# A planner that counts on its late loads three microseconds later: a one-core hybrid encoder layer

## The chip, the core and the metric

The kernel runs on one core of a Trainium2 chip. The metric is the time of one execution in microseconds on the device. A core has five engines that matter here, each with its own in-order queue of instructions: TensorE (PE), ScalarE (ACT), VectorE (DVE), GpSimd (POOL), and SyncE (SP), which in this kernel issues nearly all DMAs. An instruction that waits for a semaphore holds everything behind it on its engine.

## What is computed

One encoder layer on 512 tokens of width 1024, all in float32. The sizes are D = 1024, 16 heads of 64, a grid of 8 rows of 64 columns, a window of 8 by 16.

```python
mod = silu(c) @ w_c + b_c;  shift, scl, gate = split(mod, 3)
h = rms_norm(x, g_pre) * (1 + scl) + shift
xa, za, q, k, v, zb, ga, gb = split(h @ w_in, 8)
xa = centred_dwconv(xa, conv_w, conv_b)
y_a = ((rg_lru(xa, forward) + rg_lru(xa, backward)) * silu(za)) @ w_pa
y_b = (neighbourhood_attention(q, k, v, rpb) * silu(zb)) @ w_pb
merged = sigmoid(ga) * y_a + sigmoid(gb) * y_b
out = rms_norm(x + gate * (merged @ w_o), g_final)
```

rg_lru makes two block-diagonal sigmoid gates from xa and runs a linear scan over the tokens. The attention adds a relative-position bias and takes a softmax over the 128 keys of each query's window.

## The kernel before

Every large product is computed as three float32r matmuls: each operand is split in a high part (a cast) and a low part (the difference), and high by high, high by low and low by high are summed in one PSUM bank. So a weight tile of 128 x 1024 passes through five steps: SP loads it (wraw, 512 KB), ACT casts it (whi), POOL or DVE subtracts (wlo), PE runs 24 matmuls with it into a bank called acc, and ACT or DVE read acc. This is one projection (`proj`, L684), counted by n. Projections 9 to 32 are q, k and the gate of the eight head pairs, three each, so 12 to 14 belong to the second pair; 33 to 64 belong to four groups of the recurrent branch and of w_pb; 65 to 80 are the merge; then comes w_o.

The value columns are computed first (tiles hx). They are split, written to a scratch tensor in DRAM (vscr) and loaded again in another layout (vt), one group of loads for each two head pairs. An attention of a pair consists of scores on PE (sp), the bias added with a running minimum on DVE (p, mn; the bias tile nb is made on POOL from braw), exp on ACT (p), transposes on PE (pt), the high copy on ACT (pp, L819) and its low part on DVE (pp, L821), the product with vt on PE (pv), and three steps that take pv out (vp on ACT, vp and yt on DVE). The inverse sums (rc) are transposed on PE (mi), copied (rct), written to DRAM (rscr, L863) and loaded again spread over the partitions (rcx, L866), for the factor sz on DVE (L867).

Nothing of this order is written by hand, apart from the head of the program. Every step is recorded with an engine (or a choice of two), an estimated cost, a rank and its tiles, and a planner (`Plan`, L95 to L306) then places one step after another: it keeps a clock for each engine, estimates when each ready step could begin, and takes the one of the lowest rank that can begin within a small window of the earliest. The result is the program order of each engine. What the planner believes about a DMA is in `commit`: the transfers form one stream of 385 GB/s, and a load is there 1.9 us after its share of the stream ends (L222 and L223). What reads it is ready at that end plus the step's own `late` and a lag between engines (L239):

```python
d.t = max(d.t, end + o.late + min(self.lag(e, f) for f in d.alts) if o in d.data else s)
```

`late` moves only the moment from which readers may be placed. It changes neither the stream, nor the time at which a buffer is free. Before, only the parameters (1.9) and the two rcx loads (1.0) have a `late`.

The rank of a weight's load is n - 5, that of the bias and of the gates' weights 4 below the projection at which they stand, that of the vt loads 8 + 6g - 1.5 for the g-th group of values. A load may also be tied to the beginning of an earlier projection (`gate_of`, L681): the weight of projection n to the first matmul of n - 5.

Of the kernel before, what the change touches and what calls it, by code (L numbers as in the profile page):

```python
# [13 lines left out]
P = 128  # L14
# [14 lines left out]

NS, NW = 36, 32  # L30
WARM = 60
LIMITS = {"hx": 8, "acc": 3, "sp": 4, "pt": 2, "pv": 2, "mi": 2, "hd": 3, "gt": 4}


# [295 lines left out]
def layer(ctx, tc, x, x_t, par, w_m, w_g, bc_gate, w_v, w_in, w_blk, rpb, amask, w_pa, w_pb, w_o, g_final, out):  # L330
    nc = tc.nc
# [4 lines left out]
    dp = ctx.enter_context(tc.tile_pool(name="dp", bufs=1, space=bass.MemoryType.DRAM))  # L336
    pl = Plan({"s": NS, "w": NW, "bank": 8}, LIMITS)

    def op(eng, cost, fn, rank, name="", **kw):
        return pl.op(eng, cost, fn, HEAD.get(name, rank), name=name, **kw)  # L340
# [7 lines left out]
    def T(name, dt=F32):  # L348
        return pl.tile("s", lambda i: sb.tile([P, S], dt, tag=f"s{i}", name=nm(name)))
# [9 lines left out]
    def B(cls):  # L359
        return pl.tile(cls, lambda i: ps.tile([P, 512], F32, tag=f"b{i}", name=nm(cls)))  # L360
# [7 lines left out]
    def load(t, dst, src, rank, size, after=(), spare=0, r=(), late=0.0, name="load"):  # L368

        return op("SP", 0.45, lambda e: nc.sync.dma_start(dst(), src() if callable(src) else src), rank,  # L370
                  r=r, w=[t], after=after, spare=spare, size=size, late=late, name=name)

    def cast(o, i):

# [17 lines left out]
    def const(name, shape, dt=F32):  # L392
# [18 lines left out]
       r=[par_sb, ident], w=[pp0])  # L411
# [55 lines left out]
    for i in range(2):  # L467
        for j in range(4):
            load(xTp[j, i], whole(xTp[j, i]), x_t[i, j], -19.9 + 0.4 * i + 0.1 * j, 262144, name=f"x{i}{j}")

    rx = [C("rx", 2) for _ in range(2)]
    for i in range(2):
        st, qs = B("hd"), []
        for j in range(4):
            q = T("sq")
            qs.append(q)
            rank = -17 + 0.4 * i + 0.1 * j
            op("ACT", act(512), lambda e, i=i, j=j, q=q: nc.scalar.activation(q.ap, xTp[j, i].ap, AF.Square), rank,
               r=[xTp[j, i]], w=[q], name=f"sq{i}{j}")
            if j:  # L480
                op(("DVE", "POOL"), (dve(512), pool_(512)), lambda e, a=qs[0], q=q: ENGINE[e].tensor_tensor(a.ap, a.ap, q.ap, op=ALU.add),
                   rank, r=[q], rw=[qs[0]], lock=True, name=f"sqa{i}{j}")
# [14 lines left out]
    def fill(until, wb):  # L497
        for j in range(WARM):
            op("PE", 0.3, lambda e: nc.tensor.matmul(wb.ap[:, :P], onesc.ap, onesc.ap, start=True, stop=True), 5000 + j,
               r=[onesc], hold=[wb], until=until, name="fill")  # L500
# [10 lines left out]
    for i in range(2):  # L511
        op("ACT", act(256), cast(lambda i=i: rbs.ap[:, 256 * i:256 * i + 256], lambda i=i: rb[i].ap[:, :256]), -1 + 0.4 * i,
           r=[rb[i]], w=[rbs.part()], name=f"rbs{i}")
# [4 lines left out]
    def wv_load(k):  # L518
        if k == 0:
            for n in range(2):  # L520
                t = T("wv")
                wv[k, n] = t, (lambda t=t: t.ap)
                load(t, whole(t), w_v[k, :, n * 512:(n + 1) * 512], -17.5, 262144, spare=4, name=f"wv{k}{n}")
        else:
            t = W("wv")
            for n in range(2):
                wv[k, n] = t, (lambda t=t, n=n: t.ap[:, n * 512:(n + 1) * 512])
            load(t, whole(t), w_v[k], k - 4.5, 524288, spare=2, name=f"wv{k}")
# [226 lines left out]
    def attention(pr, q, k, z, nbt, pos):  # L755
# [24 lines left out]
        def half(bs):  # L780
# [77 lines left out]
        rct, rcx = T("rct"), T("rcx")  # L858
        scr = pl.fixed(dp.tile([8, P], F32, name=f"rscr{pr}"))
        op("PE", 0.15, lambda e: nc.tensor.transpose(rcb.ap[:8, :P], rc.ap, ident.ap), pos - 0.3, r=[rc, ident], w=[rcb], name="rcb")  # L860
        op("ACT", 0.3, lambda e: nc.scalar.activation(rct.ap[:8, :P], rcb.ap[:8, :P], AF.Copy, scale=0.5), pos - 0.3, r=[rcb], w=[rct],
           name="rct")
        op("SP", 0.5, lambda e: nc.sync.dma_start(scr.ap, rct.ap[:8, :P]), pos - 3, r=[rct], w=[scr], size=4096, name="rcs")  # L863
        for h in range(2):
            src = bass.AP(scr.ap.tensor, scr.ap.offset + h * P, [[0, 64], [2 * P, 4], [1, P]])
            load(rcx, lambda h=h: rcx.ap[H[h], :].rearrange("p (b q) -> p b q", b=4), src, pos - 3, 131072, r=[scr], name="rcl", late=1.0)  # L866
# [7 lines left out]
           name="ybl")  # L874
# [31 lines left out]
    for pr in range(8):  # L906
        n0 = len(main)
        nbt = bias(pr, n0, gate_of(n0, 2) if pr else [main[6]])
        if pr % 2 == 0:
            load_v(pr // 2, gate_of(n0, 2) if pr else [])  # L910
        q = proj(w_in[16 + pr], hhl, hll, LO_A if pr else "DVE")
        k = proj(w_in[24 + pr], hhl, hll, LO_A)
        z = proj(w_in[32 + pr], hhl, hll, LO_A)
        attention(pr, q, k, z, nbt, k[0] + 0.6)
# [199 lines left out]
    for k in range(KD):  # L1114
        raw, hi, lo = W("wo"), W("woh", F32R), W("wol", F32R)
        rank = n1 - 3 + 0.1 * k
        load(raw, whole(raw), w_o[k * P:(k + 1) * P, :], rank - 2, 524288, after=gate_of(n1, 4), spare=2, name="wo")
        for n in range(2):
            v = lambda n=n, raw=raw: raw.ap[:, n * 512:(n + 1) * 512]
            op("DVE", dve(512), lambda e, n=n, v=v: nc.vector.tensor_tensor(v(), v(), gate[n].ap, op=ALU.mult), rank,  # L1120
               r=[gate[n]], rw=[raw], lock=True, name="wog")
# [59 lines left out]
    pos = [B("acc") for _ in range(NT)]  # L1181
# [8 lines left out]
    for t in range(NT):  # L1190
        for h in range(1 + (t == NT - 1)):
            w = 256 if t == NT - 1 else 512
# [92 lines left out]
```

## Time and profile before

| what | us |
|---|---|
| median of 3 runs | 566.64 |
| lowest and highest | 566.6, 568.99 |
| the profiled execution, its own time | 569.44 |
| its span, first to last instruction | 567.6 |

The profile describes one execution. Its own time is 1.8 us longer than its span, and 2.8 us above the median. Tiles are named without their buffer numbers. A line such as L381 is that of a helper (all three-pass matmuls), so groups are told apart by their tiles. Idle time in brackets is that of the engine directly before the instruction, with what ended it. PE's instructions are pipelined: a matmul of 512 columns is listed with some 390 ns, but the next begins 0.23 us after it.

### The profile page before, as it was taken

The page shows a single profiled execution, that of the slowest core. Times are in us where ns is not written, and L with a number is a line of the kernel's source. Part 1 is how long each engine was busy: PE and PEld are TensorE (multiplying, and loading weights), DVE is VectorE, ACT ScalarE, POOL GpSimd, SP SyncE. Part 2 cuts the span into 40 slices and gives each one's busy share as a digit, 9 for nine tenths or more (in the row PEclk, how much of TensorE's full clock was granted, in tenths as well). Part 3 has the DMA queues.
Part 4 walks back from the last instruction along what each step waited for, and adds up shares of the span by engine and source line. Part 5 has one row for each costly group of instructions (what it writes and reads, how often), then busy time and mean ns, then how long its engine had stood idle before and what let it go on. Part 6 is the DMA issues. An engine that isn't in the chain of part 4 may idle for free.

```text
span 567.6 us, 7658 instructions
## 1 busy us (share of the span) xinstructions
PE 555.9 (98%) x2781; PEld 459.3 (81%) x2781; DVE 388.4 (68%) x696; ACT 322.4 (57%) x568; POOL 100.7 (18%) x95
## 2 busy tenths in 40 slices
PE   8999997999999999999999999999999999999995
PEld 8788886888888888887887887787788888888885
DVE  5899754665576667886489559749847996398323
ACT  6442545557466557579938867984894433234133
POOL 1103539184454550000000000000000000000220
PEclk9999998999999999999999999999999999999999
DMA  8993896652824721305222222223239813380002
GB/s 303 410 401 97 316 270 190 188 148 62 256 56 116 219 88 64 130 13 210 82 104 94 93 83 103 75 74 112 74 106 320 278 38 112 116 329 1 1 37 112
DMA packets 35580, 83.47 MB, mean 147 GB/s; under 512 B 3615, under 2 KB 10967, under 8 KB 35543
## 3 DMA queue, kind: packets, MB, share of 16 engines
q1 hardware_dynamic: 35264, 82.66, 44.1%
q8 instruction: 22, 0.36, 0.3%
q10 hardware_dynamic: 279, 0.32, 0.2%
q14 instruction: 15, 0.12, 0.1%
HBM read 76.65 MB, written 6.32 MB: 146 GB/s over the span
## 4 chain that ended last, share of the span: by engine, by line
PE 89%; DMA 7%; SPq 2%; DVE 1%; ACT 1%; issue 0%; ACTq 0%
PE acc L381 74%; PE hx L381 6%; DMA wv<-in_w_v_dram 3%; PE pv L381 3%; PE gt L381 2%; PE pt L813 2%; PE sp L381 2%; DMA vt<-vscr 2%; DMA wraw<-in_w_in_dram 1%; SPq L370 1%; DMA xT<-in_x_t_dram 1%; SPq L675 1%; DVE va L672 0%; DVE vl L378 0%; ACT vh L375 0%
## 5 line engine op out<-in xcount | busy, mean ns | idle before, releaser
L381 PE MATMUL acc<-hhl,whi 128*128 128x512 f32 x784 | 247.2, 396 | 0.0
L381 PEld LDWEIGHTS acc<-hhl,whi 128*128 128x128 f32 x784 | 143.8, 189 | 30.1 <-issue 1.8
L381 PE MATMUL acc<-hhl,wlo 128*128 128x512 f32 x392 | 153.5, 392 | 0.0
L381 PEld LDWEIGHTS acc<-hhl,wlo 128*128 128x128 f32 x392 | 73.9, 188 | 16.1
L375 ACT CAST whi<-wraw 128x1024 fp32r<-128x1024 f32 x72 | 74.2, 1045 | 9.1 <-DMA wraw<-in_w_in_dram 8.1
L378 POOL TENSOR_TENSOR wlo<-wraw,whi 128x1024 fp32r<-128x1024 f32 x23 | 56.5, 2457 | 73.2 <-ACT whi L375 39.0
L378 DVE TENSOR_TENSOR wlo<-wraw,whi 128x1024 fp32r<-128x1024 f32 x49 | 59.3, 1220 | 14.2 <-ACT whi L375 13.7
L1151 POOL TENSOR_TENSOR yo<-yo,gfin 128x512 f32<-128x512 f32 x6 | 8.2, 1360 | 338.0 <-ACT xr L1148 338.0
L381 PE MATMUL acc<-woh,mhl 128*128 128x512 f32 (+1 forms) x144 | 40.4, 365 | 0.0
L381 PE MATMUL acc<-yahl,whi 128*128 128x512 f32 x128 | 39.4, 389 | 0.0
L381 PE MATMUL acc<-ybhl,whi 128*128 128x512 f32 x128 | 39.4, 389 | 0.0
L1028 DVE SCALAR_TENSOR_TENSOR gm<-gm,acc 128x512 f32<-128x512 f32 x16 | 11.0, 688 | 39.4 <-PE acc L381 39.4
L799 DVE CUSTOM_DVE_ANT_0 p<-sp,nb 128x192 f32<-128x192 f32 (+1 forms) x64 | 32.7, 610 | 6.1 <-PE sp L381 6.1
L730 POOL TENSOR_TENSOR nb<-msk,braw 128x192 f32<-128x192 f32 (+1 forms) x48 | 29.0, 635 | 31.9 <-DMA braw<-in_rpb_dram 31.9
L381 PE MATMUL hx<-vh,hhl 128*128 128x512 f32 x112 | 33.7, 390 | 0.0
L806 ACT ACTIVATE p<-p,mn 128x192 f32<-128x192 f32 (+1 forms) x64 | 30.4, 478 | 5.1 <-DVE mn L799 5.0
L821 DVE TENSOR_TENSOR pp<-pt,pp 128x384 fp32r<-128x384 f32 (+1 forms) x32 | 19.8, 624 | 18.3 <-ACT pp L819 18.2
L381 PEld LDWEIGHTS acc<-woh,mhl 128*128 128x128 f32 x144 | 26.1, 189 | 4.4
L381 PEld LDWEIGHTS acc<-yahl,whi 128*128 128x128 f32 x128 | 24.0, 188 | 5.0
L381 PEld LDWEIGHTS acc<-ybhl,whi 128*128 128x128 f32 x128 | 24.0, 188 | 5.0
L381 PE MATMUL acc<-wol,mhl 128*128 128x512 f32 (+1 forms) x72 | 26.3, 365 | 0.0
L381 PE MATMUL acc<-yahl,wlo 128*128 128x512 f32 x64 | 24.9, 389 | 0.0
(202 smaller groups left out, 954.5 us busy)
## 6 DMA issues: line engine op xcount, KB each, us to landing
wraw<-in_w_in_dram SPq DMA_DIRECT2D x56, 512.0 KB, 5.8
wc<-in_w_m_dram SPq DMA_DIRECT2D x14, 512.0 KB, 9.6
vt<-vscr SPq DMA_DIRECT2D x24, 256.0 KB, 5.9
vscr<-va SPq DMA_DIRECT2D x8, 512.0 KB, 5.4
wraw<-in_w_pb_dram SPq DMA_DIRECT2D x8, 512.0 KB, 4.9
wraw<-in_w_pa_dram SPq DMA_DIRECT2D x8, 512.0 KB
wr<-in_w_g_dram SPq DMA_DIRECT2D x16, 256.0 KB, 5.8
wo<-in_w_o_dram SPq DMA_DIRECT2D x8, 512.0 KB, 4.1
```

The lines of the kernel that those rows point to most:

```text
L370: return op("SP", 0.45, lambda e: nc.sync.dma_start(dst(), src() if callable(src) else src), rank, r=r, w=[t], after=after, spare=spare, s ...
L375: return lambda e: nc.scalar.copy(o(), i()) if e == "ACT" else nc.vector.tensor_copy(o(), i())
L378: return lambda e: ENGINE[e].tensor_tensor(o(), a(), b().bitcast(F32), op=ALU.subtract)
L381: nc.tensor.matmul(o, a, b, start=first, stop=last)
L675: op("SP", 0.6, lambda e: nc.sync.dma_start(dst, a.ap.bitcast(F32).rearrange("p (g c) -> p g c", g=2)), rank - 3, r=[a], w=[vscr[n]], size ...
L730: nc.gpsimd.tensor_tensor(o, mv, view, op=ALU.subtract)
L799: nc.vector.tensor_tensor_reduce(out=o, in0=v(spv(h, e)[:, :nk]), in1=v(nb[:, h, :nk]), scale=1.0, scalar=3e38, op0=ALU.add, op1=ALU.min, ...
L806: nc.scalar.activation(pv2(i), pv2(i), AF.Exp, bias=mn.ap[:, c:c + 1], scale=-1.0, accum_out=sm.ap[:, 2 * b + h:2 * b + h + 1])
L813: nc.tensor.transpose(ptp.ap[:, j * P:(j + 1) * P], pt_.ap[:, j * P:(j + 1) * P], ident.ap)
L821: op("DVE", dve(nt * P), lambda e_, ppv=ppv, pv4=pv4: nc.vector.tensor_tensor(ppv()[:, :, 1, :], pv4(), ppv()[:, :, 0, :].bitcast(F32), op ...
L1028: op("DVE", dve(512), lambda e: nc.vector.scalar_tensor_tensor(t.ap, t.ap, 1.0, o.ap, op0=ALU.add, op1=ALU.mult), n - 1.9, r=[o], rw=[t], ...
L1151: op(("DVE", "POOL"), (dve(w), pool_(w)), lambda e: ENGINE[e].tensor_tensor(y(), y(), gfin[n].ap[:, gs], op=ALU.mult), rank + 0.1, r=[gfin ...
```

## The change

A constant SLACK = 3 is added. Loads recorded by `load` with a rank over 7.9 and no `late` of their own get it, and so does the write of the inverse sums to DRAM. The rank in that test is the one the call passes. It takes in the weights of projections 13 to 80, the bias of the second and later pairs, the vt loads of the second and later groups, the gates' weights, the gate row, g_final, w_o and the residual x. The two rcx loads keep their 1.0.

```diff
+SLACK = 3
...
     def load(t, dst, src, rank, size, after=(), spare=0, r=(), late=0.0, name="load"):
...
-                  r=r, w=[t], after=after, spare=spare, size=size, late=late, name=name)
+                  r=r, w=[t], after=after, spare=spare, size=size, late=late or SLACK * (rank > 7.9), name=name)
...
-        op("SP", 0.5, lambda e: nc.sync.dma_start(scr.ap, rct.ap[:8, :P]), pos - 3, r=[rct], w=[scr], size=4096, name="rcs")
+        op("SP", 0.5, lambda e: nc.sync.dma_start(scr.ap, rct.ap[:8, :P]), pos - 3, r=[rct], w=[scr], size=4096, late=SLACK, name="rcs")
```

The planner makes another order from it. Up to the first attention all engines' orders are as before; from the last head pair on they differ in few places. Lines of the changed kernel are two higher.

On ACT, in the first pair's attention: before, from the cast of projection 14's weight (whi_833) to the pp copies behind projection 15's (whi_907).

```order
L375 CAST whi_833<-wraw_702 128x1024
L806 ACTIVATE p_845,sm_857<-p_845,mn_846 128x192 x2
L806 ACTIVATE p_854,sm_857<-p_854,mn_855 128x256
L852 ACTIVATE sz_877<-acc_780 128x512
L806 ACTIVATE p_868,sm_857<-p_868,mn_846 128x192
L819 CAST pp_890<-pt_879 128x3x128
L806 ACTIVATE p_868,sm_857<-p_868,mn_846 128x192
L806 ACTIVATE p_854,sm_857<-p_854,mn_855 128x256
L375 CAST whi_907<-wraw_838 128x1024
L838 COPY vp_924<-pv_912 64x256
L819 CAST pp_932<-pt_920 128x3x128
L819 CAST pp_939<-pt_926 128x4x128
```

On ACT after the change, from the last exp before the first vp on; whi_921 is projection 14's cast, whi_971 that of 15, whi_999 that of 16.

```order
L808 ACTIVATE p_848,sm_851<-p_848,mn_849 128x256
L840 COPY vp_904<-pv_895 64x256
L821 CAST pp_911<-pt_900 128x3x128
L377 CAST whi_921<-wraw_702 128x1024
L821 CAST pp_928<-pt_916 128x4x128
L808 ACTIVATE p_906,sm_851<-p_906,mn_849 128x256
L840 COPY vp_904<-pv_936 64x256
L808 ACTIVATE p_906,sm_851<-p_906,mn_849 128x256
L377 CAST qh_960<-acc_866 128x512
L377 CAST whi_971<-wraw_832 128x1024
L821 CAST pp_990<-pt_977 128x4x128
L377 CAST whi_999<-wraw_837 128x1024
```

The cast of 14 went from ahead of all exps to behind the first vp and pp; that of 15 from ahead of these to behind the whole first half of the attention and the qh cast.

On POOL, same place, before: wlo_852 is projection 14's, wlo_937 that of 15; nb are the bias products of the second pair.

```order
L378 TENSOR_TENSOR wlo_803<-wraw_696,whi_796 128x1024
L378 TENSOR_TENSOR wlo_852<-wraw_702,whi_833 128x1024
L730 TENSOR_TENSOR nb_888<-msk,braw_835 128x256 x2
L730 TENSOR_TENSOR nb_902<-msk,braw_835 128x192 x2
L730 TENSOR_TENSOR nb_918<-msk,braw_835 128x192 x2
L378 TENSOR_TENSOR wlo_937<-wraw_838,whi_907 128x1024
```

And after, where wlo_965 is that of projection 14 and wlo_1026 that of 15.

```order
L380 TENSOR_TENSOR wlo_856<-wraw_696,whi_842 128x1024
L732 TENSOR_TENSOR nb_914<-msk,braw_829 128x256 x2
L732 TENSOR_TENSOR nb_933<-msk,braw_829 128x192 x2
L732 TENSOR_TENSOR nb_946<-msk,braw_829 128x192 x2
L380 TENSOR_TENSOR wlo_965<-wraw_702,whi_921 128x1024
L752 MEMSET vt_975 64x512
L752 MEMSET vt_982 64x512
L380 TENSOR_TENSOR wlo_1026<-wraw_832,whi_971 128x1024
```

Projection 14's difference changed places with the six bias products.

On SP, the second group's vt loads and what follows, before: rscr is the write of the first pair's inverse sums, rcx the load of them, wraw_1049 and wraw_1064 the weights of projections 18 and 19.

```order
L370 DMA vt_983<-vscr_87 64x1x512
L863 DMA rscr_89<-rct_992 8x128
L370 DMA vt_1008<-vscr_87 128x1x512
L370 DMA vt_1011<-vscr_87 128x1x512
L370 DMA vt_1019<-vscr_87 128x1x512
L370 DMA vt_1024<-vscr_87 128x1x512
L370 DMA vt_1032<-vscr_87 128x1x512
L370 DMA rcx_1037<-rscr_89 64x4x128 x2
L370 DMA wraw_1049<-in_w_in_dram 128x1024
L370 DMA wraw_1064<-in_w_in_dram 128x1024
```

And after.

```order
L372 DMA vt_982<-vscr_87 64x1x512
L372 DMA vt_988<-vscr_87 128x1x512
L372 DMA vt_997<-vscr_87 128x1x512
L372 DMA vt_1002<-vscr_87 128x1x512
L372 DMA vt_1013<-vscr_87 128x1x512
L865 DMA rscr_89<-rct_1018 8x128
L372 DMA vt_1028<-vscr_87 128x1x512
L372 DMA wraw_1035<-in_w_in_dram 128x1024
L372 DMA wraw_1053<-in_w_in_dram 128x1024
L372 DMA rcx_1105<-rscr_89 64x4x128 x2
```

rscr went behind four of the five vt loads, and rcx behind two weights.

On PE the same stretch has the same instructions with a few moved. Before, one more group of three matmuls of projection 12 stands ahead of the first pv, and mi and the last pt of the half stand behind the first group of projection 13. After, these read as follows from the second pv on (acc_866 is projection 12, acc_950 projection 13).

```order
L383 MATMUL pv_936<-pp_911,vt_756 128x256
L383 MATMUL acc_866<-hhl_587,whi_688 128x512 x2
L383 MATMUL acc_866<-hhl_587,wlo_718 128x512
L383 MATMUL acc_950<-hh_281,whi_842 128x512
L383 MATMUL acc_950<-hl_296,whi_842 128x512
L383 MATMUL acc_950<-hh_281,wlo_856 128x512
L383 MATMUL acc_950<-hhl_343,whi_842 128x512 x2
L383 MATMUL acc_950<-hhl_343,wlo_856 128x512
L815 MATMUL pt_977<-ident,p_906 128x128 x4
```

## Rows read from the trace of the kernel before

**Rows 1.** The head of the page: the span, and of its first part the busy time of each engine, with the share of the span and the count of instructions.

```profile
span 567.6 us, 7658 instructions
...
PE 555.9 (98%) x2781; PEld 459.3 (81%) x2781; DVE 388.4 (68%) x696; ACT 322.4 (57%) x568; POOL 100.7 (18%) x95
```

**Rows 2.** The waits of PE in the whole run, longest first: what waited for what, us in total, times, longest.

```profile
PE pv L381 <- DVE pp L821: 3.2, 1, 3.2
PE hx L499 <- POOL epsc L447: 1.5, 1, 1.5
PE hd L491 <- DVE sq L485: 0.3, 1, 0.3
```

**Rows 3.** The chain of work that ended last, 76 to 98 us: start, length, what.

```profile
79.76 6.97 DMA wraw<-in_w_in_dram
...
88.78 0.57 DVE pp L821
```

**Rows 4.** The timeline of ACT, 64 to 100 us: start, length, engine, line, operation, tiles, size, count, and the idle time before it.

```profile
76.51 1.05 ACT L375 CAST whi<-wraw 128x1024 fp32r<-128x1024 f32 x1 [2.94 <-DMA wraw<-in_w_in_dram]
...
79.16 0.60 ACT L852 ACTIVATE sz<-acc 128x512 f32<-128x512 f32 x1 [0.23 <-PE acc L381]
...
80.22 0.48 ACT L819 CAST pp<-pt 128x384 fp32r<-128x384 f32 x1
...
81.05 0.50 ACT L806 ACTIVATE p<-p,mn 128x256 f32<-128x256 f32 x1
...
86.80 1.05 ACT L375 CAST whi<-wraw 128x1024 fp32r<-128x1024 f32 x1 [5.17 <-DMA wraw<-in_w_in_dram]
87.87 0.37 ACT L838 COPY vp<-pv 64x256 f32<-64x256 f32 x1
88.27 0.97 ACT L819 CAST pp<-pt 128x384 fp32r<-128x384 f32 x2
```

**Rows 5.** The timeline of PE, 80 to 100 us, in the same columns; a row with x2 is two instructions.

```profile
82.05 0.62 PE L381 MATMUL acc<-hhl,whi 128*128 128x512 f32 x2
...
83.20 0.93 PE L813 MATMUL pt<-ident,p 128*128 128x128 f32 x7
83.89 0.71 PE L381 MATMUL acc<-hhl,whi 128*128 128x512 f32 x2
...
85.82 0.39 PE L381 MATMUL acc<-hhl,wlo 128*128 128x512 f32 x1
89.39 0.74 PE L381 MATMUL pv<-pp,vt 128*128 128x256 f32 x4 [3.19 <-DVE pp L821]
...
90.67 0.27 PE L860 MATMUL mi<-ident,rc 128*8 128x128 f32 x1
90.77 1.01 PE L813 MATMUL pt<-ident,p 128*128 128x128 f32 x4
...
94.88 0.64 PE L381 MATMUL pv<-pp,vt 128*128 128x256 f32 x4
...
96.05 0.64 PE L381 MATMUL pv<-pp,vt 128*128 128x256 f32 x4
96.53 0.62 PE L381 MATMUL acc<-hhl,whi 128*128 128x512 f32 x2
...
98.60 0.39 PE L381 MATMUL acc<-hh,whi 128*128 128x512 f32 x1
```

**Rows 6.** Busy time by stretch: from and to, length, busy time of PE, PEld, DVE, ACT and POOL, the granted clock of PE as a share of full speed, the busy share of the DMA engines, GB/s.

```profile
79.00:86.20 7.20, 7.20 (x39) 5.81 (x37) 2.29 (x6) 2.44 (x8) 2.30 (x3) 1.00 0.92 277
...
89.40:94.20 4.80, 4.80 (x19) 3.99 (x20) 3.73 (x8) 3.34 (x9) 4.24 (x4) 0.65 0.24 72
...
100.00:560.00 460.00, 460.00 (x2296) 379.02 (x2295) 313.27 (x532) 272.01 (x478) 64.80 (x56) 1.00 0.36 118
```

**Rows 7.** The timeline of POOL, 55 to 130 us.

```profile
77.63 2.39 POOL L378 TENSOR_TENSOR wlo<-wraw,whi 128x1024 fp32r<-128x1024 f32 x1 [1.60 <-ACT whi L375]
84.74 0.68 POOL L730 TENSOR_TENSOR nb<-msk,braw 128x256 f32<-128x256 f32 x1 [4.71 <-DMA braw<-in_rpb_dram]
85.60 2.75 POOL L730 TENSOR_TENSOR nb<-msk,braw 128x256 f32<-128x256 f32 x5 [0.19 <-DMA braw<-in_rpb_dram]
88.31 2.37 POOL L378 TENSOR_TENSOR wlo<-wraw,whi 128x1024 fp32r<-128x1024 f32 x1
```

**Rows 8.** The timeline of SP's DMA issues, 55 to 110 us; the length is that of the issuing instructions, not of the transfers.

```profile
77.40 1.63 SPq L370 DMA_DIRECT2D braw<-in_rpb_dram  x2
...
92.35 0.30 SPq L863 DMA_DIRECT2D rscr<-rct  x1
...
95.97 1.27 SPq L370 DMA_DIRECT2D rcx<-rscr  x2
97.29 2.22 SPq L370 DMA_DIRECT2D wraw<-in_w_in_dram  x3
```

**Rows 9.** Of DVE: the first reader of rcx in its timeline, and the line for rcx in its list of waits over the whole run (us in total, times, longest).

```profile
103.17 0.69 DVE L867 TENSOR_TENSOR sz<-sz,rcx 128x512 f32<-128x512 f32 x1 [2.94 <-DMA rcx<-rscr]
...
DVE sz L867 <- DMA rcx<-rscr: 6.7, 4, 3.2
```

**Rows 10.** Near the end: the first matmul of the last product (timeline of PE), and the last split of the merged tile (timeline of DVE).

```profile
517.24 0.39 PE L381 MATMUL acc<-woh,mhl 128*128 128x512 f32 x1
...
525.84 0.68 DVE L378 TENSOR_TENSOR mhl<-gm,mhl 128x512 fp32r<-128x512 f32 x1
```

## The prediction

> **What bounds the kernel now.** I read the page first, then TensorE's own waits, then the chain of waits and the timelines around the one place that stood out. The page has PE busy 98% of a span of 567.6 us, with the other engines at 18 to 68% [rows 1]. Matmul spans overlap, so 98% is not a measure of peak, but it says that PE hardly ever has nothing to do. What PE waits for in the whole run says where: one wait of 3.2 us for DVE's pp before a pv matmul, beside it 1.5 us at the very start, 0.3 for the third and less for the last [rows 2]. So, past the head, there is a single hole to win, and a re-ordering that fills it can bring no more than the hole is worth, unless PE does less work (it does not).
>
> The chain shows what the hole is made of [rows 3]: the load of a weight tile issued at 79.76 took 6.97 us to land, ACT's whi cast waited for it until 86.80, and behind it on ACT stood vp and two pp copies of the attention; DVE's pp ended the wait of PE at 89.39. The ACT timeline says the same from the other side: last exp at 81.05, then 5.17 us of waiting for wraw with the vp and pp copies queued behind it [rows 4]. The pt transposes that these pp copies read had gone out on PE at 83.20 and the following 0.93 us [rows 5]: ACT was held by the order alone. It is projection 15's cast that blocks (whi_907 in the order), while PE is only at the end of projection 12.
>
> What the hole costs is more than 3.2 us, since the rows behind it are slow. From 85.82 to 94.88 PE issued 1 + 3 + 9 matmuls of 512 columns, four pv, one mi and four pt. Undisturbed, nine matmuls take 98.60 - 96.53 = 2.07 us (0.23 each), four pv 96.53 - 96.05 = 0.48, seven pt 83.89 - 83.20 = 0.69 (0.39 for four), mi 90.77 - 90.67 = 0.10 [rows 5]: 13 x 0.23 + 0.48 + 0.39 + 0.10 = 3.96. It took 9.06, so 5.1 are lost: 3.3 standing (86.05 to 89.39) and 1.8 behind it, where the granted clock averages 0.65 over 89.4 to 94.2, that is, mostly the 1.2 GHz level; from 100 to 560 it is 1.00 [rows 6].
>
> **The change part by part.** No instruction is added or removed; the plan alone believes that readers of a late load can begin 3 us later, so each such reader falls behind work that is ready sooner. DMA issue, buffers and tile sizes stay.
>
> *ACT at the hole.* whi of projection 14 (whi_921) now follows the vp and pp copies of the first half, and whi of projection 15 (whi_971) follows the exps, a vp and the qh cast. I walk the new order with the old durations [rows 4]: vp, pp, exp and whi take 0.37, 0.37 to 0.49, 0.45 to 0.50 and 1.05. zt ends at 79.76, pp waits for pt as before (80.22), three exps follow to 82.0. On PE pv now comes one set of three matmuls earlier, at 82.05 to 82.53; vp to 83.0, pp to 83.4, whi_921 (landed by 76.51) to 84.4, pp to 84.95, exp to 85.4. PE's next pv stands two sets behind the pt block and begins near 85.4, its pp and DVE's share being done by 84.2; vp to 86.3, exp to 87.0, qh (end of projection 12, 86.5 + 0.4) to 87.5, whi_971 (landing 86.73, so no wait) to 88.5. PE reaches the pt block that reads that exp at 86.54 + 2 x 0.69 = 87.9, 0.9 after it. pp_990 behind whi_971 is copied at 89.1 and subtracted by 89.75; PE wants it at 88.3 + 2 x 0.69 + 0.10 + 0.48 + 0.69 = 91.0. Every margin is 0.9 or more: the hole closes and nothing stands in its place. Value: 5.1 of this execution.
>
> *POOL.* wlo of projection 14 falls behind six bias products, which wait for braw until 84.74 and 85.60 and end at 88.31 [rows 7]; one wlo takes 2.37 to 2.39, so it ends at 90.7. Before it was done by 80.0. PE begins projection 14 at 91.0 + 0.48 + 9 x 0.23 = 93.55: 2.9 to spare. wlo of 15 ends near 94.2, wanted near 100.4. Cost: nothing, but this cover is new (below).
>
> *SP.* rscr leaves its place ahead of four vt loads. Before, SP stood at it until 92.35, the vt loads and three weights behind it [rows 8]. Now the vt loads go as their buffers come free, projections 18 and 19's weights go before the rcx loads, and rcx follows the gate of weight 19 (the first matmul of projection 14, 93.55): issued 94.0 to 95.3. Before, rcx's second issue ended at 97.24 and its reader began at 103.17 [rows 8, 9], 5.9 later; by that it lands at 101.2. Its reader now stands behind six score operations and sz on DVE, which I put near 102, and directly ahead of a pp that PE waits for. Margin about 1; the price is bounded by 0 and the longest wait for rcx that the trace has, 3.2 [rows 9]. I take 0.
>
> *The rest of the attention (100 to 250).* ACT, DVE and PE are re-ordered pair by pair in the same manner. PE waited nowhere there before [rows 2], so nothing can be won; what could be lost is such a pp. I take 0, and keep the 3.2 as the bound.
>
> *The end.* The w_o loads' readers move back by up to 3 us. The last mhl is done at 525.84 + 0.68 = 526.5; PE meets it 63 matmuls of 0.23 after 517.24, at 531.7 [rows 10]. Margin 5.2 before, at least 2.2 after: nothing. The recurrent stage swaps gate casts with weight casts, off the path.
>
> **The sum.** Profiled execution: 569.44, of which 567.6 span, minus 5.1: 564.3. That execution is 2.8 above the median of the runs (566.64), whose third run is at 568.99. If the 2.8 lie elsewhere, the median loses the whole 5.1: 561.5. If all 2.8 are in the hole (a shorter wait, no slow stretch), it loses 2.3 and comes to 564.3. The slow stretch (1.8) alone missing gives 563.3. I take the middle of the two ends, 3.7: 562.9.
>
> The Trainium skill, "TensorE: Matmul & The Clock Gate", Part 1, says that where the clock gate switches is not tied to the kernel's start, so that the same kernel shows different numbers of slow matmuls from run to run. This trace is one execution and can't show that; by the rule the 1.8 would be in some runs and not in others, for which 563.3 would be the time.
>
> **Rivals.**
> 1. *The hole is small in the runs that count.* For it: the profiled execution is 2.8 slower than two runs of three, and the hole is its only visible loss. Against: tracing may itself cost, and the landing that makes the hole is 7 us behind its issue in a stretch where the DMA engines are 92% busy [rows 6]. 564.3, a gain of 0.4%.
> 2. *A new wait takes its place: rcx ahead of pp.* For it: readers of rcx did wait four times before [rows 9], and now PE's pv is right behind. Against: rcx was asked for 1.3 to 2 us sooner relative to the trace, its reader stands later. Up to 3.2 less the margin of 1: 565.1.
> 3. *Slower: wlo of projection 14 on POOL.* The six bias products in front of it wait for braw, issued from 77.40, landed 84.74 and 85.60. If braw lands L later, PE stands L - 2.9, and after a hole of that size comes the slow stretch (1.8). From L = 2.9 it costs, and at L = 7.7 it gives 562.9 + 4.8 + 1.8 = 569.5. Against: the landing would have to take twice its 7 us, while the queue ahead of it is as before.
> 4. *The order doesn't matter:* ACT still stands at a cast that hasn't landed. The new order has only landed tiles ahead of the copies by the walk above. 566.6.
>
> **Chances.** Forecast (561.5 to 563.8) 0.62; rival 1 0.20; rival 2 0.08; rival 3 0.07; rival 4 0.03. The first has the ends of the carried loss as its own range. The whole range goes down to 561.2 (5.1 and a little for spread) and up to 566.0, which leaves out rivals 3 and 4 and little else. A change under 0.5% (2.8 us) can't be told from none: faster takes the forecast and the upper edge of rival 1, 0.65; within, 0.27; slower, 0.08.
>
> **What would show it.** Right: PE's list of waits has no wait for pp near 86; the granted clock is 1.00 from 80 to 100; ACT's casts of 14 and 15 begin behind vp and pp, and whi_971 waits little or not at all for wraw; projection 14 begins near 93.6 instead of 98.6; from there all of PE lies 5 us earlier. Wrong: a PE wait on pp after an rcx wait of DVE (rival 2), a PE wait on wlo near 94 with POOL held by braw (rival 3), or a profile 5 us shorter with a median only 2 us lower (rival 1). If PE has no wait at all and the time is still above 565, the reading of the one hole is wrong.

## The result, and the profile after

| | before | after |
|---|---|---|
| median, 7 runs each, us | 567.12 | 564.44 |
| lowest and highest | 565.85, 569.61 | 564.13, 565.2 |
| the profiled execution, its own time | 569.44 | 564.48 |
| its span | 567.6 | 562.4 |

The ratio is 0.9947, with a 95% interval from 0.9927 to 0.9968: the change makes the kernel faster, by 2.7 us in these medians and by 5.2 us between the two profiled spans. The forecast was 562.9, in a range from 561.2 to 566.0. After also spreads far less: 1.1 us between its lowest and highest run, where before has 3.8.

The head of the page and PE's waits after, which answer to [rows 1, 2]:

```profile
span 562.4 us, 7654 instructions
...
PE 553.9 (98%) x2781; PEld 457.9 (81%) x2781; DVE 386.7 (69%) x696; ACT 322.8 (57%) x568; POOL 99.7 (18%) x95
```

```profile
PE hx L501 <- POOL epsc L449: 1.5, 1, 1.5
PE hx L383 <- POOL vl L380: 0.3, 1, 0.3
PE hd L493 <- DVE sq L487: 0.2, 1, 0.2
```

The wait of 3.2 us for pp has gone from the list, and nothing has come into its place. The share of PE is still 98%: a share can't show a gain of 1%, the list of waits does. ACT's timeline around the place, after, to be read against [rows 4]:

```profile
82.59 0.37 ACT L840 COPY vp<-pv 64x256 f32<-64x256 f32 x1 [0.64 <-PE pv L383]
82.99 0.48 ACT L821 CAST pp<-pt 128x384 fp32r<-128x384 f32 x1
83.36 1.05 ACT L377 CAST whi<-wraw 128x1024 fp32r<-128x1024 f32 x1
84.31 0.59 ACT L821 CAST pp<-pt 128x512 fp32r<-128x512 f32 x1
...
86.80 0.56 ACT L377 CAST qh<-acc 128x512 fp32r<-128x512 f32 x1
87.27 1.05 ACT L377 CAST whi<-wraw 128x1024 fp32r<-128x1024 f32 x1
88.42 0.59 ACT L821 CAST pp<-pt 128x512 fp32r<-128x512 f32 x1
```

The cast at 87.27 is projection 15's. It starts later than before (86.80), and yet it has no bracket: its tile had landed while ACT did the copies that used to stand behind it. PE's timeline [rows 5] now runs through:

```profile
85.23 0.63 PE L383 MATMUL pv<-pp,vt 128*128 128x256 f32 x4
...
87.79 0.60 PE L815 MATMUL pt<-ident,p 128*128 128x128 f32 x4
...
90.90 0.64 PE L383 MATMUL pv<-pp,vt 128*128 128x256 f32 x4
...
93.44 0.39 PE L383 MATMUL acc<-hh,whi 128*128 128x512 f32 x1
```

The last row is the start of projection 14, which was at 98.60: 5.16 us earlier. The stretches of [rows 6], with one for the old hole, 86.20 to 89.40; before's row for that one stands first:

```profile
86.20:89.40 3.20, 0.01 (x2) 0.01 (x1) 0.62 (x2) 2.55 (x5) 3.20 (x6) 1.00 0.67 209
```

```profile
79.00:86.20 7.20, 7.20 (x42) 6.13 (x42) 3.88 (x9) 5.54 (x15) 2.18 (x4) 1.00 0.92 295
86.20:89.40 3.20, 3.20 (x18) 2.63 (x17) 2.53 (x6) 3.07 (x7) 3.20 (x4) 1.00 0.98 228
89.40:94.20 4.80, 4.80 (x27) 4.03 (x26) 2.02 (x5) 3.17 (x6) 4.69 (x5) 1.00 0.83 233
100.00:560.00 460.00, 455.95 (x2265) 375.63 (x2263) 311.47 (x532) 272.65 (x477) 64.46 (x56) 1.00 0.36 117
```

PE issues 18 matmuls in the 3.2 us in which it issued none, and 27 in place of 19 in the next stretch, at a granted clock of 1.00 in place of 0.65. The 4.05 us that the last row lacks are its end, where PE has finished. POOL, SP and the reader of rcx [rows 7 to 9]:

```profile
83.90 3.60 POOL L732 TENSOR_TENSOR nb<-msk,braw 128x256 f32<-128x256 f32 x6 [7.84 <-DMA braw<-in_rpb_dram]
87.46 2.41 POOL L380 TENSOR_TENSOR wlo<-wraw,whi 128x1024 fp32r<-128x1024 f32 x1
```

```profile
91.21 0.44 SPq L865 DMA_DIRECT2D rscr<-rct  x1
91.97 0.54 SPq L372 DMA_DIRECT2D vt<-vscr  x1
93.06 1.09 SPq L372 DMA_DIRECT2D wraw<-in_w_in_dram  x2
97.99 1.27 SPq L372 DMA_DIRECT2D rcx<-rscr  x2
```

```profile
SPq L372 <- DMA rscr<-rct: 6.2, 5, 3.8
```

```profile
102.53 0.69 DVE L869 TENSOR_TENSOR sz<-sz,rcx 128x512 f32<-128x512 f32 x1 [0.30 <-DMA rcx<-rscr]
```

```profile
511.96 0.39 PE L383 MATMUL acc<-woh,mhl 128*128 128x512 f32 x1
```

Projection 14's difference on POOL ends at 89.87, 3.6 us before PE wants it. The rcx loads go out at 97.99, 2.0 us later than before, because SP stood 3.8 us for the landing of rscr; their reader waited 0.30 for them. The first matmul with w_o is at 511.96 in place of 517.24, 5.28 earlier: nearly all of the gain is made by projection 14.

So three lengths, read off the first score product (sp) of the first and of the second pair in PE's timeline, tell the kernels here apart: the head up to the first, *the place* between the two, and the rest from there to the end of the span. Before these rows are

```profile
74.50 0.36 PE L381 MATMUL sp<-kh,qh 64*128 64x192 f32 x2
...
102.09 0.36 PE L381 MATMUL sp<-kh,qh 64*128 64x192 f32 x2
```

and after

```profile
74.38 0.36 PE L383 MATMUL sp<-kh,qh 64*128 64x192 f32 x2
...
96.94 0.36 PE L383 MATMUL sp<-kh,qh 64*128 64x192 f32 x2
```

| profiled execution | head | place | rest | clock over the run |
|---|---|---|---|---|
| before | 74.50 | 27.59 | 465.6 | 0.995 |
| before, again (a4) | 73.92 | 25.13 | 466.5 | 0.999 |
| after | 74.38 | 22.56 | 465.4 | 0.997 |
| a1, 15's weight alone | 74.87 | 22.51 | 466.6 | 0.997 |
| a2, all but the place | 74.23 | 26.31 | 466.8 | 0.993 |
| a3, slack 10 | 73.90 | 23.16 | 472.8 | 0.997 |
| b1, before with extra loads | 74.67 | 30.41 | 465.7 | 0.992 |
| b2, after with extra loads | 73.81 | 22.51 | 465.7 | 0.998 |
| b3, 15's weight and the sums | 73.75 | 22.53 | 471.8 | 0.995 |
| b4, slack 6 | 75.03 | 22.54 | 475.3 | 0.992 |
| c1, after with rcx 4 | 74.49 | 22.56 | 465.8 | 0.996 |
| c2, 15's weight and rcx 4 | 73.37 | 22.51 | 465.6 | 0.998 |
| c3, slack 6 with rcx 6 | 74.69 | 22.53 | 466.3 | 0.999 |
| c4, before with rcx 4 | 74.70 | 26.85 | 465.5 | 0.993 |

A place without a hole is 22.5 us, a rest without one 465.5 or so. The head's spread (73.4 to 75.0) lies ahead of every edit: PE has the same 357 instructions in the same order there in all of them. The places hold the same work on PE too, with one exception: a3 has 66 matmuls of 512 columns (acc) in it, all others 75. Nine at 0.23 are 2.1 us that PE does behind it there, so on equal work a3 has a place of 25.2 and a rest of 470.8.

### The profile page after: what moved, and what is told of

It reads as the page before. It is cut to its first block, busy times and chain, and to the rows that moved or that the text cites. A ratio compares the mean times of both kernels' runs of the same rounds, so it can differ in the third digit from the quotient of the medians.

```text
span 562.4 us, 7654 instructions
## 1 busy us (share of the span) xinstructions
PE 553.9 (98%) x2781; PEld 457.9 (81%) x2781; DVE 386.7 (69%) x696; ACT 322.8 (57%) x568; POOL 99.7 (18%) x95
## 4 chain that ended last, share of the span: by engine, by line
PE 96%; DMA 2%; DVE 0%; SPq 0%; POOL 0%; ACT 0%; issue 0%; POOLq 0%
PE acc L383 78%; PE hx L383 8%; PE pv L383 3%; PE sp L383 2%; PE gt L383 2%; PE pt L815 2%; DMA wv<-in_w_v_dram 1%; DMA xT<-in_x_t_dram 1%; SPq L372 0%; POOL vl L380 0%; PE mi L383 0%; PE mi L862 0%; DVE yo L1174 0%; ACT vh L377 0%; DVE yo L1142 0%
## 5 line engine op out<-in xcount | busy, mean ns | idle before, releaser
L801 DVE CUSTOM_DVE_ANT_0 p<-sp,nb 128x192 f32<-128x192 f32 (+1 forms) x64 | 31.2, 613 | 16.7 <-PE sp L383 16.7
```

The source lines that it names most:

```text
L801: nc.vector.tensor_tensor_reduce(out=o, in0=v(spv(h, e)[:, :nk]), in1=v(nb[:, h, :nk]), scale=1.0, scalar=3e38, op0=ALU.add, op1=ALU.min, ...
```

## The experiments

My theory was that of the prediction: one cast, projection 15's, held the copies that PE waited for. The rivals were that the gain comes from the other places that the slack moves, or that more slack gives more; the first results then put a second wait beside the first, that for rcx.

**a1_w15_only.** Slack on one load alone:

```diff
-                  r=r, w=[t], after=after, spare=spare, size=size, late=late, name=name)
+                  r=r, w=[t], after=after, spare=spare, size=size, late=late or 3.0 * (name == 'w15'), name=name)
```

> The kernel before, with 3 us of slack for readers of projection 15's weight alone, nothing else. Theory A (the whole gain is the one hole in front of the second pv of the first pair): PE has no wait for pp, the span is 562 to 563 us, the ratio to before 0.993 to 0.997, as with the full change. Rival B (the hole is only part, the rest of the re-ordering from 100 us on carries some of it): PE has no wait for pp there, but the time stays 1 us or more above that of the full change. Rival C (the order at that place doesn't matter, the gain is chance): no difference to before, ratio 0.998 to 1.002.

Measured: 565.56 us, ratio 0.996 (0.9945 to 0.9974). The place is 22.51, the hole gone. The ratio is inside theory A's range; the span, 564.0, is 1 us above it, as rival B had it. The rest is 1.1 longer than before's, and PE's list and DVE's timeline show why:

```profile
PE pt L813 <- ACT p L806: 0.4, 1, 0.4
```

```profile
100.43 0.69 DVE L867 TENSOR_TENSOR sz<-sz,rcx 128x512 f32<-128x512 f32 x1 [5.02 <-DMA rcx<-rscr]
```

DVE stands 5.02 us at the reader of rcx, with the second pair's score operations queued behind it; exp on ACT is late from it, and so are the transposes on PE. One load's slack makes the hole's gain, but about 1 us falls to a wait that the old hole had covered.

**a2_all_but_the_place.** The reverse: 3 us for all loads of rank over 12.4 (from projection 18's weight on) and for the write of the sums, none for the weights of 13 to 17:

```diff
-                  r=r, w=[t], after=after, spare=spare, size=size, late=late, name=name)
+                  r=r, w=[t], after=after, spare=spare, size=size, late=late or 3.0 * (rank > 12.4), name=name)
...
-size=4096, name="rcs")
+size=4096, late=3.0, name="rcs")
```

> Slack of 3 us for all loads of rank over 12.4 and for the write of the inverse sums, none for the weights of projections 13 to 17 and the biases of the second and third pair. The order on ACT up to the cast of projection 16 is that of before. Theory A: PE waits for pp near 86 as before, ratio to before 0.998 to 1.002. Rival B: faster than before by 0.2% or more though the hole is still there. If the later re-ordering costs something that the full change hides, slower by 0.2% or more, with a new wait of PE after 100 us.

Measured: 570.12 us, ratio 1.0038 (1.0021 to 1.0055), the third case of the expectation. The hole is there, a wait of 1.93, and a second one follows, from the matmul at 152.30 to the next at 153.71. It stands behind another reader of rcx. The cast that makes the first, and the reader and PE's wait of the second:

```profile
85.27 1.05 ACT L375 CAST whi<-wraw 128x1024 fp32r<-128x1024 f32 x1 [3.91 <-DMA wraw<-in_w_in_dram]
```

```profile
149.67 0.69 DVE L867 TENSOR_TENSOR sz<-sz,rcx 128x512 f32<-128x512 f32 x1 [2.88 <-DMA rcx<-rscr]
...
153.71 0.74 PE L381 MATMUL pv<-pp,vt 128*128 128x256 f32 x4 [1.03 <-DVE pp L821]
```

The rest of the change brings nothing by itself, and here costs.

**a3_slack_10** (`SLACK = 10`).

> SLACK 10 in place of 3. The cast of projection 13 now stands on ACT behind all exps, the vp, two pp copies and the qh cast of the first pair, and PE's program puts the rest of that attention (pt, mi, four groups of pv) in one piece ahead of projection 13. Theory A (what counts is only whether PE has released work in its order): PE waits inside that piece for pp and then for wlo of projection 13, which POOL can begin only after that cast, 3 to 6 us in all, with a stretch of half clock behind: span 566 to 570, no gain over before or a loss. Rival D (more slack is never worse, since the loads land early): span 562 to 563 as with 3.

Measured: 571.88 us, ratio 1.0069 (1.0046 to 1.0093). PE's waits past the head:

```profile
PE pv L381 <- DVE pp L821: 3.5, 2, 2.3
...
PE sp L381 <- DVE kl L763: 1.0, 2, 0.5
PE acc L381 <- DVE wol L378: 0.6, 2, 0.4
PE acc L381 <- ACT mhl L375: 0.4, 1, 0.4
```

The longest of them is inside the place:

```profile
89.43 0.74 PE L381 MATMUL pv<-pp,vt 128*128 128x256 f32 x4 [2.33 <-DVE pp L821]
```

More slack is not better. The wait for pp inside the piece came as theory A had it, that for projection 13's difference didn't. The place looks nearly closed (23.16), but by the nine matmuls that are missing from it, it is 2.7 long of a closed one, and the rest loses some 5.3 and not 7.4. Part of that is 1.14 at 109.90, behind a reader of rcx that waited 2.4, and part is at the end, at w_o; the rest of it isn't traced.

**a4_before_again.** Before, unchanged, in one more execution.

> The kernel before once more, for a second execution with a trace. Theory A with a landing that varies: the wait of PE for pp is another than 3.2 us, and the span differs from 567.6 by as much as the wait and the slow stretch do: about 562.5 plus the wait plus 0 to 1.8. Rival E (the hole is always 3.3 and the spread of before has another source): wait 3.1 to 3.3, whatever the span.

Measured: 567.32 us, a place of 25.13. The hole is a wait of 2.3, and no slow stretch follows it, but the rest is 0.9 longer than before's: the reader of rcx waits, and transposes and a pv at 104 to 108 come late behind it, as in a1:

```profile
PE pv L381 <- DVE pp L821: 2.3, 1, 2.3
```

```profile
101.69 0.69 DVE L867 TENSOR_TENSOR sz<-sz,rcx 128x512 f32<-128x512 f32 x1 [4.50 <-DMA rcx<-rscr]
```

So the same program loses 5.0 at the place in one execution and 2.6 + 1 in another.

**b1_before_late_landing and b2_after_late_landing.** Both kernels with two extra transfers of 512 KB, DRAM to DRAM, issued just ahead of projection 15's weight, so that it should land late:

```diff
+        def go(e):
+            for j in range(2 * (name == "w15")):
+                nc.sync.dma_start(dp.tile([P, D], F32, name=f"extra{j}"), w_in[40 + j])
+            nc.sync.dma_start(dst(), src() if callable(src) else src)
```

> The kernel before, with two more transfers of 512 KB (from the weights to unused DRAM) issued by SP right in front of projection 15's weight; the order of all computing instructions is that of before, so the weight lands 3 to 6 us later and all that is behind it in the queue as well. Theory A (the hole is the landing, passed on by ACT's order): PE's wait for pp grows to 5 to 9 us, with a stretch of half clock behind it; ratio to before 1.006 to 1.015. Rival E (the hole has another source than the landing): the wait stays near 2 to 3.3.

> The changed kernel with the same two extra transfers in front of projection 15's weight. Theory A: the cast of 15 now has 1 us in hand before PE meets the pp behind it, so a landing 3 to 6 us later costs 1 to 5 us, each time 3 us or more less than in the kernel before with the same transfers: about 565.5 to 569, that is a ratio of 0.995 to 1.004 to the unchanged kernel before. Rival F (the change protects against any late landing): no PE wait, 564.5. Rival G (it protects against none, the hole only fell on a luckier order): as much lost as in the kernel before with the same transfers.

Measured: b1 570.67 us, ratio 1.0039 (1.0019 to 1.0059); b2 564.71 us, ratio 0.9938 (0.9919 to 0.9958). Projection 15's cast, in the order before and after:

```profile
88.71 1.04 ACT L380 CAST whi<-wraw 128x1024 fp32r<-128x1024 f32 x1 [6.91 <-DMA wraw<-in_w_in_dram]
```

```profile
86.79 1.05 ACT L382 CAST whi<-wraw 128x1024 fp32r<-128x1024 f32 x1
```

In b1 the cast begins 1.9 us later, PE's wait is 4.9 and the place 30.41 (in this execution, the slowest of its ten). In b2 ACT doesn't wait, and the place is 22.51. That the tile was late there too is in the trace's record of the load's semaphore: it landed at 86.76, just ahead of the cast, where after has 85.72. Counted from the first sp that is 1.6 later than in after; in b1 it is 1.7 later than before. Both prices had been expected higher, for a landing 3 to 6 us later. b2 came out as rival F had it: no PE wait, and 564.5 forecast. What follows is the direction: the new order doesn't feel this landing, up to that delay. All that ACT had in hand was used up by it, and a later landing wasn't tried.

**b3_w15_and_sums.** a1's edit, and `late=3.0` for the write of the sums.

> Slack for projection 15's weight and for the write of the inverse sums, nothing else. What the run with that weight alone lost against the full change (a wait of pt for p at 102, 0.9 us, behind a wait of 5 us of DVE for rcx that stood ahead of the scores) should be gone, since sz stands behind the scores here. But sz of a later pair stands ahead of scores and a pp as in the run without the place, which had a hole of 1.4 us near 152. If the slack on the weights of 13 to 17 has nothing to do with that hole, it shows here too: span 563.3 to 564, ratio 0.994 to 0.997. If it was a matter of when PE came there, no hole: span 562.4, as with the full change.

Measured: 566.59 us, ratio 0.9975 (0.9951 to 0.9999). The first hole is closed (22.53), and the rest is 6.3 longer in the profiled execution. That one, 570.17, is 3.6 above the median of its runs, and its span of 568.0 is outside both branches of the expectation; seven of the twelve runs have spans of 563.5 to 564.7, near the first. Against b2 on the same chip (564.71) the median loses 1.9. PE's wait, and what it stands behind on DVE:

```profile
107.61 0.74 PE L381 MATMUL pv<-pp,vt 128*128 128x256 f32 x4 [2.94 <-DVE pp L821]
```

```profile
104.13 0.69 DVE L867 TENSOR_TENSOR sz<-sz,rcx 128x512 f32<-128x512 f32 x1 [4.81 <-DMA rcx<-rscr]
```

This is rival 2 of the prediction, in another order: a reader of rcx waits, and a pp that PE wants is behind it.

**b4_slack_6** (`SLACK = 6`).

> SLACK 6 in place of 3. The cast of 13 goes behind the exps, that of 14 behind the first half of the attention, 15 and 16 behind rct and the last pp. Theory A: what PE meets next is still ready in time (wlo of 13 by 85, needed at 86.4; wlo of 14 by 91, needed at 93.5), so 562 to 563 us of span, ratio 0.993 to 0.997, as with 3. Rival H (each us of slack beyond the lateness costs): between the results with 3 and with 10, that is a ratio of 1.000 or so, with PE waits for pp or wlo near 86 to 95.

Measured: 574.18 us, ratio 1.0109 (1.0072 to 1.0146), slower than with 10, so my theory's expectation failed, and with it rival H's, which put it between 3 and 10. The place is closed (22.54). PE waits twice for pp, and DVE's list of waits names rcx:

```profile
PE pv L381 <- DVE pp L821: 6.2, 2, 4.0
```

```profile
DVE sz L867 <- DMA rcx<-rscr: 10.5, 3, 5.9
```

The two long ones are these, each with a wait of PE for pp behind it (2.2 at 151.88, 4.0 at 199.86):

```profile
148.23 0.69 DVE L867 TENSOR_TENSOR sz<-sz,rcx 128x512 f32<-128x512 f32 x1 [3.91 <-DMA rcx<-rscr]
...
196.38 0.69 DVE L867 TENSOR_TENSOR sz<-sz,rcx 128x512 f32<-128x512 f32 x1 [5.92 <-DMA rcx<-rscr]
```

a2, a3, b3 and b4 have one thing in common: the rcx loads keep `late=1.0` while other loads or the write of the sums are raised. The last four kernels test that for 3 and 6 us; for 10 it wasn't tried.

```diff
-pos - 3, 131072, r=[scr], name="rcl", late=1.0)
+pos - 3, 131072, r=[scr], name="rcl", late=4.0)
```

**c1_after_rcx_4** is after with this edit, **c2_w15_and_rcx_4** is a1 with it, **c4_before_rcx_4** is before with it, and **c3_slack_6_rcx_6** is b4 with 6.0 there.

> The changed kernel, with the two rcx loads' late raised from 1.0 to 4.0 and nothing else. The planner then puts one pp and one pair of score operations ahead of the first reader of rcx (sz) on DVE. Theory A (the change has won what there is in this stretch: no PE wait is left but that at the head): no difference, 564 to 565.5, ratio to before 0.993 to 0.998; the waits of DVE for rcx fall from 1.3 us in all to under 0.5. Theory R (readers of rcx still cost something that PE's list of waits doesn't show): up to 1 us less, ratio 0.991 to 0.993. Theory S (any further re-ordering is a draw, and can open a hole elsewhere): a PE wait of 1 us or more and a ratio over 0.998.

> Before, with 3 us for projection 15's weight alone and 4.0 in place of 1.0 for the two rcx loads: the two waits that I hold for the whole gain, and nothing else of the change. Theory A (two waits: the cast of 15 ahead of the pp copies, and the reader of rcx ahead of the scores): as good as the change, ratio 0.9935 to 0.997, and no PE wait over 0.3 us past the head, where with the weight alone there were about 0.9 us lost behind the rcx wait. Theory B (the other loads' slack is needed too): ratio over 0.997, with a PE wait elsewhere.

> The changed kernel with SLACK 6 (it was 1.011 of before, with two PE waits on pp, 2.6 and 4.4 us, both behind a reader of rcx) and 6.0 for the two rcx loads. Theory R (what makes larger slacks slow is that the rcx loads alone keep 1.0): both holes gone, no DVE wait for rcx over 1.5 us, and 564 to 567, ratio 0.993 to 1.000. Theory O (believing loads later than they land costs by itself, since work that is ready is passed over): still a ratio of 1.004 or more, with PE waits on something other than pp behind rcx.

> Before, with 4.0 in place of 1.0 for the two rcx loads and no other slack. Up to the first pair's attention the order is as before, so the hole ahead of the second pv stays (a PE wait on pp of 2 to 5 us near 86, ended by the cast of projection 15). Theory A: the hole is most of it, so the ratio is 0.997 to 1.001; the waits of DVE for rcx fall from 6.7 us in all to under 2. Rival (the rcx waits are most of what the change removes in the runs that count): ratio under 0.996.

| | median, us | ratio | interval |
|---|---|---|---|
| c1 | 564.26 | 0.9926 | 0.9912 to 0.994 |
| c2 | 564.02 | 0.9922 | 0.9908 to 0.9937 |
| c3 | 565.0 | 0.9937 | 0.9922 to 0.9953 |
| c4 | 569.28 | 1.0017 | 0.9998 to 1.0036 |

DVE's list of waits has no line for rcx in any of the four. In c3 the readers that had waited in b4 are

```profile
151.88 0.68 DVE L867 TENSOR_TENSOR sz<-sz,rcx 128x512 f32<-128x512 f32 x1
...
195.58 0.68 DVE L867 TENSOR_TENSOR sz<-sz,rcx 128x512 f32<-128x512 f32 x1
```

c3 takes away all of b4's loss: 574.18 and a rest of 475.3 become 565.0 and 466.3. So slack 6 was slow because of the rcx loads' own 1.0, and not because loads were held later than they land; 0.8 of its rest is left over. c2 has two `late` values changed and nothing else, no PE wait past the head, and is as fast as c1, which has the whole change: these two values bring the whole gain. Its ratio is below the 0.9935 that theory A gave as the lower end. c4 shows that the second alone is worth nothing: its hole is still there,

```profile
PE pv L381 <- DVE pp L821: 2.7, 1, 2.7
```

and its ratio is above theory A's 1.001, though the interval reaches down into its range. In c1 the change gains nothing that can be told apart: its median is inside after's range of runs, as theory A had it. Its ratio is 0.0004 under A's range, and so in that of theory R, but against other runs of before than after's. After itself didn't run beside c1 and c2 on one chip.

## Why the prediction was right, and where it was off

*The hole and its mechanism: right.* Projection 15's cast, ahead of copies whose input was ready, was the whole of it (a1 closes it with one load's slack). The walk through the new order was within 0.2 us on the three pv and pt that mattered: pv at 85.23 (walked 85.4), pt at 87.79 (87.9), pv at 90.90 (91.0), projection 14 at 93.44 (93.55). The hole's price, 5.1, was worked out from 3.3 standing and 1.8 slow; the place shrank by 5.03.

*POOL (rival 3): right.* The difference ended at 89.87 where 90.7 was walked, with 3.6 to spare. No run made braw land later, so the price that the rival had isn't shown. *The end: right.* No wait for w_o at 3 us; at 10 there are some (a3).

*The carried loss: mis-sized in this comparison.* The step said that the median would lose between 2.3 and 5.1, and took 3.7. It lost 2.7, and 2.2 against the 566.64 from which the forecast was carried. The runs point to how much of the hole an execution has. Of the 62 runs of before that stood beside a1 to c4, 38 have a granted clock of 0.995 or less over the run and a mean of 568.88; 24 have 0.996 or more and a mean of 567.25. All runs of after, and of a1, b2, c1, c2 and c3, are at 0.996 or more. In the traces, before has the slow stretch and 0.995, a4 has none and 0.999. By that sign the stretch is in some three of five of before's runs; and the hole varies without it too (2.57 in a4). The Trainium skill, "TensorE: Matmul & The Clock Gate", Part 1, has it that the gate's switching isn't tied to the kernel's start and differs from run to run; the runs agree. Before's median also differs between the sets of runs: 567.12 with the result, then 567.73, 569.22 and 567.99, on three chips. b2 and c1, which have the new order at the place, were at 564.71 and 564.26 beside the last two: there the gain was 4.5 and 3.7. The time forecast, 562.9, was below all of these medians: it was carried from 566.64, the median of three runs, and before's larger sets have more; as a ratio to that median it is 0.9934, inside the measured interval.

*Rival 1* gave 564.3, and the time came out there: inside the whole range, but outside the forecast's own 561.5 to 563.8, which had the higher chance. The sign that the prediction gave for it, a profile 5 us shorter with a median only 2 us lower, is what came (5.2 and 2.7). What it said, a hole smaller than that of the profiled execution in the runs that count, fits this comparison's median.

*SP and rcx: wrong in a step that cost nothing.* The loads were walked to go at 94.0 to 95.3 and went at 97.99: the walk had the gate of weight 19, and left out that rcx must wait for the landing of rscr, which had moved back. The margin of 1 was −0.3, and that this cost nothing was luck. The bound of 3.2 was none: readers of rcx waited 5.02 in a1, 4.81 in b3 and 5.92 in b4, and in b3 the rest was 6.3 longer in the profiled execution.

*"Nothing can be won from 100 to 250": off by about 1 us.* PE's list before had no wait there, since the hole had put PE's next stretch late enough for rcx's landing: before's rest, 465.6, is as short as after's. With the hole smaller (a4) or closed alone (a1) this second wait shows. After has it at 0.30, c2 not at all.

## What to carry to other kernels

A list of waits names the first of several that overlap: when a wait is taken away, walk on to the next late landing and ask what stands behind its reader, before calling the rest of the run free. In a planner, believe each kind of late load as late as it lands; raising most of them and leaving one can make that one's readers the next to block (b4 against c3: 574.18 and 565.0). And where a stall's size depends on a landing, carry it from the profiled execution to the median with the spread of several runs, not of three.

## What the runs showed of the hardware

PE's granted clock fell after one short wait and not after a longer one. After the wait of 1.93 us in a2, and after that of 2.34 in a4, both at 86 to 88, the next 4 us read

```profile
88.00:92.00 4.00, 4.00 (x16) 3.26 (x17) 3.30 (x8) 3.33 (x9) 3.55 (x4) 0.58 0.35 127
```

```profile
88.00:92.00 4.00, 4.00 (x23) 3.39 (x24) 3.31 (x8) 3.31 (x9) 3.54 (x4) 1.00 0.37 134
```

with 16 matmuls at 0.58 (mostly the 1.2 GHz level) in the first and 23 at 1.00 (the 2.4 GHz level) in the second. a2's place is the longer one by it, 26.31 against 25.13. So a wait of some 2 us was followed by a slow stretch in one execution and not in another; what decides it wasn't tried.

Small transfers can land late. In after, rscr, a write of 4 KB issued at 91.21, was what the rcx loads on SP waited for until 97.99, 6.8 us later. In before the same write, issued at 92.35, had landed by 93.89, 1.5 us later, by the trace's record of its semaphore; the DMA engines were 0.24 busy from 89.4 to 94.2 there, and 0.83 in after. And rcx's reader could begin 4.5 us after the issue in after, and 8.9 after it in b3 (95.25 to 104.13). Which of the other transfers in flight makes the difference wasn't tried.
